# Nearest-neighbour upsampling by two: two loads instead of three, other store sizes, a first copy on one engine

## The chip, the cores and the metric

The kernel runs on one core of a Trainium2 chip. The metric is the device time of one execution in microseconds (us); for a run of several executions the median is given. Beside it there is a profile of one execution, taken by the hardware profiler, with a span of its own that is a little shorter than the measured time.

## The reference

```python
def setup_inputs():
    batch, channels, h, w = (16, 64, 64, 64)
    return {'x': np.random.randn(batch, channels, h, w).astype(np.float32), 'scale_factor': 2}

def reference(x, scale_factor):
    ...
    for i in range(new_h):
        for j in range(new_w):
            src_i = i // scale_factor
            src_j = j // scale_factor
            result[:, :, i, j] = x[:, :, src_i, src_j].copy()
    return result.astype(np.float32)
```

Each pixel of 1024 images of 64 x 64 is written four times, as a square of 2 x 2. The input has 16.78 MB, the output 67.11 MB. There is no arithmetic, only moving and repeating.

## The kernel before

**Layout.** The 65,536 input rows (64 floats, 256 bytes each) are dealt to the 128 partitions of the on-chip memory: R = 512 consecutive rows to each (L173). An input row becomes two output rows of 128 floats, 1024 bytes, so that a partition's share of the output is one contiguous piece of 512 KB in memory off the chip.

**One tile.** Everything lives in one tile `mem` (L187): the whole input `xt` at its end, 512 rows per partition, and FREE = 79 output blocks (WF = 79 x 256 elements) in front of it. Each block is one input row expanded to 256 elements. The expanded rows of a store are put either at the front of the tile (even stores) or at an address that ends where the unread input begins (odd stores, L206), over input rows that have been copied already.

**Loads.** The input comes in three transfers issued by SyncE (L195): 32 rows per partition (`HEAD`, 8 KB in a piece), 256 rows (64 KB) and 224 rows (56 KB). `begin_before_barrier` moves the first EARLY load instructions ahead of the barrier at the program's start, so that they are issued at once.

**The loop** (L204 to L216) runs over `rows`, the nine store sizes. For store n of k rows, VectorE expands the first kv rows (L213), ScalarE the rest (L214), both reading each element twice along the row and each row twice by a step of zero. SyncE issues the store (L215) once both have finished. In store 0 VectorE takes all rows but one, in the others 9/16 of them, rounded down.

**What waits for what.** All loads and stores are issued by SyncE and go through one queue, q1, in order. The copy for store n needs its input loaded, and its place free: store n-2 has used the same part of the tile, so it must have landed. An odd store's place also covers input rows, so its copy waits for earlier copies that read these. The store waits for the copies alone. While store n-1 is being written, the copy for store n can run. `close_early` arranges the wait for the last store at the end; it takes the last store's semaphore from the program and is not touched by the edit.

Of the kernel before, what the change touches and what calls it, by code (L numbers as in the profile page):

```python
# [6 lines left out]

EARLY = 3  # L10


def begin_before_barrier(nc):
# [5 lines left out]
    sp = mybir.EngineType.SP  # L19
    loads = [i for i in body.instructions if i.engine == sp][:EARLY]  # L20
    for load in loads:
# [132 lines left out]
@with_exitstack  # L154
def kernel(
    ctx: ExitStack,
    tc: tile.TileContext,
    x: bass.AP,
    scale_factor: int,
    out: bass.AP,  # L160
):
    nc = tc.nc
    nc.at_finalize(begin_before_barrier)
    nc.at_finalize(close_early)
    P = nc.NUM_PARTITIONS
    s = int(scale_factor)
    B, C, H, W = x.shape
    R = B * C * H // P
    fdt = x.dtype

    xp = x.rearrange("b c h w -> (b c h) w").rearrange("(p r) w -> p r w", p=P)  # L173
    op = out.rearrange("b c (h hd) w -> (b c h) (hd w)", hd=s).rearrange(
        "(p r) w -> p r w", p=P
    )

    rows = [54, 38, 52, 63, 52, 64, 63, 63, 63]
    GROW = s * s
    FREE = 79
    WF = FREE * GROW * W
    assert sum(rows) == R
    mem_pool = ctx.enter_context(tc.tile_pool(name="mem", bufs=1))
    mem = mem_pool.tile([P, WF + R * W], fdt, name="mem")  # L187
    xt = mem[:, WF:].rearrange("p (r w) -> p r w", r=R)

    HEAD = 32
    cuts = [0, HEAD, R // 2 + HEAD, R]
    for lo, hi in zip(cuts, cuts[1:]):
        nc.sync.dma_start(out=xt[:, lo:hi], in_=xp[:, lo:hi])  # L195

    def expanded(r0, r1):
        return (
            xt[:, r0:r1].unsqueeze(2).unsqueeze(4).to_broadcast([P, r1 - r0, s, W, s])
        )  # L200

    r0 = 0
    before = (0, 0)
    for n, k in enumerate(rows):  # L204
        size = k * GROW * W
        at = 0 if n % 2 == 0 else WF + r0 * W - size  # L206
        assert at >= before[1] or at + size <= before[0]
        before = (at, at + size)
        u = mem[:, at : at + size].rearrange(
            "p (k a w b) -> p k a w b", k=k, a=s, w=W  # L210
        )
        kv = k - 1 if n == 0 else k * 9 // 16
        nc.vector.tensor_copy(out=u[:, :kv], in_=expanded(r0, r0 + kv))  # L213
        nc.scalar.copy(out=u[:, kv:], in_=expanded(r0 + kv, r0 + k))  # L214
        nc.sync.dma_start(out=op[:, r0 : r0 + k, :], in_=u)  # L215
        r0 += k  # L216

# [34 lines left out]
```

## Time and profile before

| | |
|---|---|
| time, median of 3 runs | 197.24 us (196.97 to 197.29) |
| span of the profiled execution | 195.9 us (195.86) |
| moved by DMA | 83.89 MB, mean 428 GB/s over the span |
| load 1, 1024 KB | issued at 0.0, lands 4.8 us later |
| load 2, 8192 KB | issued at 0.43, lands 23.7 us later |
| load 3, 7168 KB | issued at 0.9, lands 40.1 us later |
| store 0, 6912 KB | issued at 38.57, lands 18.8 us later |
| VectorE (DVE) | 9 copies, 78.6 us |
| ScalarE (ACT) | 9 copies and a table load, 46.5 us |

In the profile DVE is VectorE, ACT ScalarE, POOL GpSimd and SP SyncE; SPq and DVEq are their instruction queues. A landing is the moment at which all 16 DMA engines have reported a transfer as done. A copy is named by its size, so 128x8960 is 35 rows of 256 elements on 128 partitions. The row of digits gives the busy share of each fortieth of the span in tenths, 9 for 90% or more. The chain of waits follows the execution back from its last instruction, at each step to whatever released it. DMA packets are counted in the stretch in which they begin, so that the share of a short stretch can lie above one, and that of the next one below.

### The profile page before, as it was taken

To read this page: it belongs to the slowest core of one execution; us is meant where nothing else is said; L and a number is where in the kernel's file an instruction comes from. 1 tells how busy PE (TensorE), PEld (TensorE's weight loads), DVE (VectorE), ACT (ScalarE), POOL (GpSimd) and SP (SyncE) were. 2 spreads that over 40 slices of the span, in tenths; PEclk is the share of its full clock that TensorE was granted. 3 is DMA by queue.
4 is the path that set the end of the run, shared out by engine and by line. 5 is a ranking of instruction groups with operands and counts; after the bars stand their busy time and mean duration, and the time that the engine had idled before them with its cause. 6 is when DMAs were issued, how large, how long until landed. Compare 5 with 4: busy or idle time off the path is not lost.

```text
span 195.9 us, 102 instructions
## 1 busy us (share of the span) xinstructions
DVE 78.6 (40%) x9; ACT 46.5 (24%) x10; POOL 0.2 (0%) x4
## 2 busy tenths in 40 slices
DVE  0000099990029399078008106930692079100000
ACT  2000000160027093074910006665000074000000
POOL 0000000000000000000000000000000000000000
DMA  9999989889899989899999899999999999999994
GB/s 428 428 428 428 402 375 550 386 361 542 361 435 397 540 348 522 348 422 422 448 417 500 370 500 428 428 428 428 422 422 422 435 435 514 461 435 448 435 422 211
DMA packets 1728, 83.89 MB, mean 428 GB/s; under 512 B 192, under 2 KB 192, under 8 KB 192
## 3 DMA queue, kind: packets, MB, share of 16 engines
q1 hardware_dynamic: 1728, 83.89, 99.2%
HBM read 16.78 MB, written 67.11 MB: 428 GB/s over the span
## 4 chain that ended last, share of the span: by engine, by line
DMA 60%; DVE 25%; issue 0%; SPq 0%; DVEq 0%
DMA out_dram<-mem 48%; DVE mem L213 25%; DMA mem<-in_x_dram 12%; SPq L195 0%; DVEq L213 0%; SPq L215 0%
## 5 line engine op out<-in xcount | busy, mean ns | idle before, releaser
L213 DVE COPY mem<-mem 128x8960 f32<-128x8960 f32 (+4 forms) x9 | 78.6, 8745 | 88.7 <-DMA out_dram<-mem 64.5
L214 ACT COPY mem<-mem 128x7168 f32<-128x7168 f32 (+3 forms) x9 | 45.2, 5027 | 115.6 <-DMA out_dram<-mem 74.1
L214 ACT ACT_TABLE_LOAD x1 | 1.3, 1283 | 1.7 <-PEq L233 1.7
L233 POOL MEMSET const-uint8-127<- 128x1 uint8 x1 | 0.1, 102 | 0.0
L233 POOL MEMSET const-bfloat16-1.0<- 128x1 bf16 x1 | 0.1, 101 | 0.0
L233 POOL MEMSET const-float32-0.0<- 128x1 f32 x1 | 0.1, 98 | 0.2 <-issue 0.2
L233 POOL MEMSET const-float32-1.0<- 128x1 f32 x1 | 0.1, 98 | 0.0
## 6 DMA issues: line engine op xcount, KB each, us to landing
out_dram<-mem SPq DMA_DIRECT2D x4, 8064.0 KB, 28.5
out_dram<-mem SPq DMA_DIRECT2D x2, 6656.0 KB, 22.9
mem<-in_x_dram SPq DMA_DIRECT2D x1, 7168.0 KB, 40.1
out_dram<-mem SPq DMA_DIRECT2D x1, 6912.0 KB, 18.8
out_dram<-mem SPq DMA_DIRECT2D x1, 4864.0 KB, 24.7
mem<-in_x_dram SPq DMA_DIRECT2D x1, 1024.0 KB, 4.8
mem<-in_x_dram SPq DMA_DIRECT2D x1, 23.7
out_dram<-mem SPq DMA_DIRECT2D x1, 30.0
```

Of the source, the lines that this page charges most:

```text
L213: nc.vector.tensor_copy(out=u[:, :kv], in_=expanded(r0, r0 + kv))
L214: nc.scalar.copy(out=u[:, kv:], in_=expanded(r0 + kv, r0 + k))
L233: nc = _bacc.Bacc("TRN2", target_bir_lowering=False, num_devices=1)
```

## The change

```diff
-EARLY = 3
+EARLY = 2
...
-    rows = [54, 38, 52, 63, 52, 64, 63, 63, 63]
+    rows = [60, 34, 55, 61, 55, 62, 62, 62, 61]
...
-    HEAD = 32
-    cuts = [0, HEAD, R // 2 + HEAD, R]
+    cuts = [0, R // 2, R]
     for lo, hi in zip(cuts, cuts[1:]):
         nc.sync.dma_start(out=xt[:, lo:hi], in_=xp[:, lo:hi])
...
-        kv = k - 1 if n == 0 else k * 9 // 16
+        kv = k if n == 0 else k * 7 // 16
         nc.vector.tensor_copy(out=u[:, :kv], in_=expanded(r0, r0 + kv))
-        nc.scalar.copy(out=u[:, kv:], in_=expanded(r0 + kv, r0 + k))
+        if kv < k:
+            nc.scalar.copy(out=u[:, kv:], in_=expanded(r0 + kv, r0 + k))
         nc.sync.dma_start(out=op[:, r0 : r0 + k, :], in_=u)
```

The loads become two of 256 rows per partition, 64 KB in a piece, both ahead of the barrier. The nine stores have 60, 34, 55, 61, 55, 62, 62, 62 and 61 rows. VectorE copies all 60 rows of store 0, and 14, 24, 26, 24, 27, 27, 27 and 26 rows of the others; ScalarE copies 20, 31, 35, 31, 35, 35, 35 and 35. Before, VectorE had 53, 21, 29, 35, 29, 36, 35, 35 and 35 rows, ScalarE 1, 17, 23, 28, 23, 28, 28, 28 and 28. Bytes, the order of the stores and the engine that issues them are as they were. In the changed kernel the loads stand in line 194, VectorE's copy in line 212; ScalarE's copy and the stores keep lines 214 and 215.

## The prediction

> **What bounds the kernel now.** I read the page first: its shares and slices, then the chain of waits, the copies by shape, and the transfers over short stretches.
>
> ```profile
> DVE 78.6 (40%) x9; ACT 46.5 (24%) x10; POOL 0.2 (0%) x4
> ...
> DMA  9999989889899989899999899999999999999994
> ...
> q1 hardware_dynamic: 1728, 83.89, 99.2%
> ```
>
> The compute engines work 40% and 24% of the span; the DMA engines work in all of it (99.2%), and the only low slice is the last. So the first suspicion is that the bytes set the time. The chain seems to say otherwise (25% VectorE), so I check whether a copy in it ever leaves the queue empty:
>
> ```profile
> 0.43 23.67 DMA mem<-in_x_dram
> ...
> 24.20 14.30 DVE mem L213
> ...
> 38.57 18.80 DMA out_dram<-mem
> ...
> 57.46 7.90 DVE mem L213
> ...
> 65.43 19.09 DMA out_dram<-mem
> ```
>
> Load 2 lands at 0.43 + 23.67 = 24.10. Load 1 (the issues' view: 1024 KB, 4.8 us to landing) lands at about 4.76. So 8.389 MB took 24.10 - 4.76 = 19.34 us, or 433.7 GB/s. Load 3, issued at 0.9, lands 40.1 us later, at 41.0. Store 0 was issued at 38.57 and landed at 57.37; its 7.078 MB need 16.32 us at that rate, so it moved from 41.05 on: the moment the loads ended. The VectorE link in the chain is the last condition for the issue, not for the data, which queued behind load 3. The same for store 2: issued at 65.43, 3.5 us before store 1 landed (copy 3, which waits for store 1, began at 68.97).
>
> All bytes at that rate: 83.89 MB / 433.7 GB/s = 193.43 us. Load 1 alone took 4.76 us for 1.049 MB, which need 2.42: 2.34 us are the start and the landing. 193.43 + 2.34 = 195.77 against a span of 195.86. All eleven joints between the twelve transfers thus cost about 0.1 us together, some 0.01 each. The span is start-up plus bytes. The start in short stretches (columns: stretch, length, VectorE, ScalarE, GpSimd, clock, DMA share, GB/s; a packet counts where it begins):
>
> ```profile
> 0.00:1.00 1.00, 0.00 (x0) 0.00 (x0) 0.20 (x4) 1.00 0.00 0
> 1.00:2.00 1.00, 0.00 (x0) 0.27 (x1) 0.00 (x0) 1.00 1.04 238
> ```
>
> Nothing moves in the first 1.0 us. In the next one 238 GB/s start where 433.7 would fit: (433.7 - 238) x 1 us = 0.196 MB, 0.45 us of lost flow, a ramp.
>
> **The change, part by part.** The sum is made on the span of 195.86; the median, 197.24, lies 1.38 above it, and I carry that over.
>
> *One load less.* The same 16.78 MB come in two transfers. One joint falls away: 0.01 us. The question is the ramp, since the first transfer now has rows of 64 KB instead of 8 KB, which no row shows at the start. Bounds: if the ramp belongs to the small rows, it goes, -0.45 us; if it lasts as long as each DMA engine's first row, a row of 64 KB (8.389 MB in 8 rows per engine and 19.34 us: 2.42 us each) at 238/433.7 of the rate takes 4.41 us, a loss of 2.0 instead of 0.45, +1.5 us. I take nearly the old ramp, as a thing of the first microsecond: -0.1, since in the stretch from 2 to 4 us the same small rows already flow at 528 GB/s as counted. SyncE spends 0.38 us to issue the first load and 0.43 on the others: +0.05 at most. Load 1 of the changed kernel lands at 2.34 + 19.34 = 21.7, load 2 at 41.0.
>
> *The first copy on VectorE alone, 60 rows.* It waited for loads 1 and 2 (24.10); now for load 1 only (21.7). Its duration comes from this:
>
> ```profile
> L213 DVE COPY mem<-mem 128x8960 f32<-128x8960 f32 x4 | 37.9, 9486 | 33.9 <-DMA out_dram<-mem 33.9
> ...
> L214 ACT COPY mem<-mem 128x5888 f32<-128x5888 f32 x2 | 10.2, 5098 | 24.4 <-DMA out_dram<-mem 24.4
> L213 DVE COPY mem<-mem 128x5376 f32<-128x5376 f32 x1 | 5.7, 5744 | 0.0
> L213 DVE COPY mem<-mem 128x9216 f32<-128x9216 f32 x1 | 5.0, 4961 | 11.1 <-DMA out_dram<-mem 11.1
> ```
>
> Copies of 21, 29, 35 and 53 rows fit 0.14 us + 1.043 ns an element; the one of 36 rows takes half (0.523 ns). So 60 rows (15360 elements) take 16.2 us or 8.2 us: store 0 is issued at 37.9 or 29.9, before 38.57 either way, and its data wait for load 2 until 41.0. No gain, no loss. The cover is load 2; were it gone, the copy's whole length would show.
> By the Trainium skill (VectorE: DVE Perf Modes, "What auto-detection actually checks") a one-source copy uses both ports when the outermost dimensions are even or equal; the trace agrees: only the even count, 36, is at half time. By it the copies of 60, 14, 24, 26, 24 and 26 rows run fast and VectorE's 78.6 us fall to about 46; the end stays.
>
> *ScalarE's one row goes (0.41 us), its table load moves.* The added condition leaves nine VectorE and eight ScalarE copies. The compiled order puts the wait for load 1 on the table load, so its 1.28 us come at 21.7 instead of 1.73; behind it stands only ScalarE's copy 1, which waits for VectorE's copy 0 anyway (its output covers the input rows copy 0 reads). Hidden by copy 0: 0.
>
> *New sizes and 7/16 on VectorE.* ScalarE's rows fit 0.19 us + 0.833 ns an element: 31 rows 6.8 us, 35 rows 7.7 us. VectorE's odd 27 rows take 7.35 us, so ScalarE ends most copies. Copy n+2 starts when store n lands and is covered by store n+1. The thinnest cover is store 1, now 34 rows, 4.456 MB, 10.3 us. Store 0 lands at 41.0 + 18.1 = 59.1; copy 2 ends at 59.1 + 0.1 + 6.8, store 2 is issued at 66.1, store 1 lands at 69.4: 3.3 us ahead, where 3.5 was enough before, and 2.4 (38.57 against 41.0) at store 0. Every later store has at least 8 us (copy 3: issue 77.3, store 2 lands 86.0). SyncE issues the stores in the same order, nothing is moved past another. Cost: 0.
>
> *Sum:* -0.01 - 0.1 + at most 0.05 is about -0.1: a span near 195.8 and a time of 197.1.
>
> **Rivals.**
> 1. *The ramp was the small rows'.* All of it goes: -0.46 us, 196.8. For it: the low rate is seen only in load 1, the one transfer with 8 KB rows. Against: it is also the only one that meets idle engines.
> 2. *The ramp lasts as long as the first row.* +1.5: 198.7. It decides from an excess of 0.4 us. For it: no 64 KB row ever began on idle engines here. Against: small rows reached full flow within the first few, at one time for all.
> 3. *Store 2 comes late.* Fast VectorE copies beside a ScalarE copy are not in the trace (copy 5's two parts ran at 103.63 and 92.58). Should ScalarE stand still for VectorE's 3.35 us of copy 2, it ends at 69.4 and store 2 is issued as store 1 lands. The engines then sit idle for at least the 1.0 us from issue to first packet, at most the 2.4 us proven enough: +1.4 taken, 198.5. The price starts where copy 2 exceeds about 7.7 us (0.9 us of spare cover). Against: slow VectorE copies left ScalarE alone (6.17 us beside one, 6.16 without).
> 4. *Each load pays its start again.* Then the load taken out is worth load 1's 2.34 us: 194.9. The trace speaks against it: eleven joints in 0.1 us.
> The Trainium skill (DMA: Bandwidth & Descriptors, "Anatomy of one DMA") names about 2.0 us fixed for each transfer, by which it would be about 195.2; transfers that queue behind one another do not pay it in this trace.
>
> **How the numbers follow.** Forecast 0.57, rival 1 0.19, rival 2 0.11, rival 3 0.06, rival 4 0.02, and 0.05 for a loss of unknown place. No change means within 0.2%, 0.39 us (196.85 to 197.63), about what a measurement of this kernel can tell. Forecast: same, save 0.01 on the slow side by scatter (the three runs spread over 0.32 us). Rival 1 ends on the border; I count it faster, with rival 4: 0.21. Slower: 0.11 + 0.06 + 0.05 + 0.01 = 0.23. Same: 0.56. The range: 196.5 holds rival 1 with scatter, 198.3 the smaller half of rivals 2 and 3; outside stay rival 4 and their larger half, about 0.15. The forecast's own range is 196.9 to 197.4.
>
> **What would show it.** The DMA row stays at 9 but for the ends; load 1 lands near 21.7, load 2 near 41.0; the 128x15360 copy takes 8.2 us; store 0 lands near 59.1 wherever it is issued; store 2 is issued 3 us before store 1 lands; VectorE falls to 46 us with the same span. Wrong would be: a first load landing after 22.1 (rival 2) or before 21.4 (rival 1), a ScalarE copy of 128x7936 above 7.7 us or a low DMA slice near 69 us (rival 3), or a span under 195.2.

## The result and the profile after

| | before | changed |
|---|---|---|
| time, median of 5 runs | 197.24 us (196.97 to 197.42) | 198.37 us (198.20 to 198.50) |
| span of the profiled execution | 195.86 | 196.96 |
| VectorE, ScalarE busy | 78.6, 46.5 | 46.1, 57.6 |
| first copy's input lands | 24.10 | 21.75 |
| store 0 issued, lands | 38.57, 57.37 | 29.96, 60.45 |

The ratio is 1.0057, with a 95% interval of 1.0045 to 1.0070: slower by 1.1 us, where about -0.1 was forecast and the range ended at 198.3.

The page of the changed kernel (shares, slices, queue), and the first steps of its chain of waits (start, length, what):

```profile
DVE 46.1 (23%) x9; ACT 57.6 (29%) x9; POOL 0.2 (0%) x4
...
DMA  9999999999999989889998998999999999999994
...
q1 hardware_dynamic: 1584, 83.89, 99.2%
```

```profile
0.00 21.75 DMA mem<-in_x_dram
...
21.77 8.17 DVE mem L212
...
29.96 30.49 DMA out_dram<-mem
...
60.47 6.82 ACT mem L214
...
67.31 20.05 DMA out_dram<-mem
```

By the page nothing is lost: the DMA engines are busy 99.2% of the span in both kernels, with 99.2% of a longer one here. The chain shows where the time is. Load 1 lands at 21.75 (21.7 forecast), the first copy takes 8.17 us (8.2), store 0 is issued at 29.96 (29.9). But it lands at 29.96 + 30.49 = 60.45, where the bytes give 59.1. Behind it all goes at the old rate: store 0's landing to the span's end are 136.5 us, and stores 1 to 8 have 59.24 MB, which need 136.6 at 433.7 GB/s. So the whole difference lies between load 1's landing and store 0's, in 38.7 us in which the queue was never empty.

The issue of load 2 (us from issue to landing) narrows it further:

```profile
mem<-in_x_dram SPq DMA_DIRECT2D x1, 41.9
```

Issued at 0.42, load 2 lands at 42.3 instead of 41.0 or 41.1. The load became late, not the store. The packets in stretches of 2 us around the joint of loads and stores, the kernel before first, the changed one second (stretch, length, VectorE, ScalarE, GpSimd, clock, DMA share, GB/s):

```profile
36.00:38.00 2.00, 2.00 (x1) 0.00 (x0) 0.00 (x0) 1.00 0.86 373
38.00:40.00 2.00, 2.00 (x2) 1.43 (x1) 0.00 (x0) 1.00 0.99 430
40.00:42.00 2.00, 2.00 (x1) 2.00 (x1) 0.00 (x0) 1.00 1.03 442
```

```profile
36.00:38.00 2.00, 0.00 (x0) 0.00 (x0) 0.00 (x0) 1.00 0.83 229
38.00:40.00 2.00, 0.00 (x0) 0.00 (x0) 0.00 (x0) 1.00 0.99 295
40.00:42.00 2.00, 0.00 (x0) 0.00 (x0) 0.00 (x0) 1.00 1.14 492
```

The packets that begin from 38 to 40 keep the DMA engines as busy as before (0.99), but carry 295 GB/s, not 430. The packet records behind these lines give each piece of a transfer, one partition's share of it on one DMA engine, with its start and length. Such a piece is called a row here: load 2 has 128 rows of 64 KB, eight for each engine. From 30 us on, every row of load 2 takes 2.42 or 2.43 us but the last of each engine, which takes 3.3 to 4.0. Both compute engines are idle at that time. A busy share says that packets were open, not that bytes flowed at the full rate.

### The profile page after: what moved, and what is told of

It reads as the page before. It is cut to its first block, busy times and chain, and to the rows that moved or that the text cites. A ratio compares the mean times of both kernels' runs of the same rounds, so it can differ in the third digit from the quotient of the medians.

```text
span 197.0 us, 96 instructions
## 1 busy us (share of the span) xinstructions
DVE 46.1 (23%) x9; ACT 57.6 (29%) x9; POOL 0.2 (0%) x4
## 3 DMA queue, kind: packets, MB, share of 16 engines
q1 hardware_dynamic: 1584, 83.89, 99.2%
## 4 chain that ended last, share of the span: by engine, by line
DMA 66%; ACT 15%; DVE 4%; issue 0%; ACTq 0%
DMA out_dram<-mem 55%; ACT mem L214 15%; DMA mem<-in_x_dram 11%; DVE mem L212 4%; ACTq L214 0%
## 5 line engine op out<-in xcount | busy, mean ns | idle before, releaser
L214 ACT COPY mem<-mem 128x8960 f32<-128x8960 f32 (+2 forms) x8 | 56.4, 7045 | 88.0 <-DMA out_dram<-mem 81.2
L212 DVE COPY mem<-mem 128x6912 f32<-128x6912 f32 (+4 forms) x9 | 46.1, 5135 | 117.4 <-DMA out_dram<-mem 95.6
```

## The experiments

Two things had changed at this joint: the last load's rows (64 KB instead of 56), and how long store 0 had stood in the queue when the loads ended (some 12 us instead of 2.5). Theory A blames the waiting store, theory C the loads.

To compare the runs I take one number from the chain of each: store 0's landing, less the landing that released the first copy, less the bytes between them (last load and store 0) at 433.7 GB/s. It is 57.37 - 24.10 - 33.24 = 0.03 us for the kernel before and 60.45 - 21.75 - 37.47 = 1.23 for the changed one; "the loss at the joint" below. Ratios are against the kernel before, timed on the same chip, with their 95% interval.

**1. The kernel before with a fast first copy.** Only the first copy changes, from 53 rows and 1 row to an even 54 on VectorE.

```diff
-        kv = k - 1 if n == 0 else k * 9 // 16
+        kv = k if n == 0 else k * 9 // 16
...
+        if kv < k:
```

> The kernel before, with its three loads and its sizes; only the first copy changes: all 54 rows on VectorE, an even count, so about 7.4 us instead of 14.3, and store 0 is issued near 31.6 instead of 38.57. Theory A (a store that stands in the queue well before the loads end makes the last load rows slow): load 3 lands about 1.2 us later, near 42.2, the span is near 197.1, the time near 198.4. Theory C (the loads of 64 KB rows at the end are what is slow, whenever the store is issued): load 3 lands at 41.0, span 195.9, time 197.2.

198.32 us, ratio 1.0054 (1.0039 to 1.0069). From its chain:

```profile
0.42 23.90 DMA mem<-in_x_dram
...
31.81 26.87 DMA out_dram<-mem
```

The issue of load 3 (us from issue to landing, 40.1 in the kernel before):

```profile
mem<-in_x_dram SPq DMA_DIRECT2D x1, 7168.0 KB, 41.4
```

The same loads, the same sizes, a copy that ends 7 us earlier, and load 3, issued at 0.9, lands at 42.3, where theory A had 42.2 and theory C 41.0. Store 0 lands at 58.68, not at 57.37: a loss at the joint of 1.11 us. One line of the diff accounts for nearly all of the change, and it is one that makes an engine faster.

**2. The changed kernel with a slow first copy.** The reverse.

```diff
-        kv = k if n == 0 else k * 7 // 16
+        kv = k - 1 if n == 0 else k * 7 // 16
```

> The changed kernel with its two loads and its sizes; only the first copy changes: 59 rows on VectorE, an odd count, and one row on ScalarE, so about 15.9 us instead of 8.2, and store 0 is issued near 37.7 instead of 29.96. Theory A: the last rows of load 2 take 2.4 us again, load 2 lands near 41.0, the span is near 195.8, the time near 197.1. Theory C: nothing changes, span 197.0, time 198.4.

197.69 us, ratio 1.0021 (1.0012 to 1.0030). Store 0, issued at 37.90, lands at 59.62; the loss at the joint is 0.25. This fits theory A, with a remainder: an issue 0.7 us earlier than in the kernel before still costs something. (The profiled execution, 197.46, was the fastest of the ten, so the usual loss is rather larger.)

**3. The changed kernel with three loads.** All three are issued ahead of the barrier, as in the kernel before.

```diff
-EARLY = 2
+EARLY = 3
...
-    cuts = [0, R // 2, R]
+    cuts = [0, 32, R // 2 + 32, R]
```

> The changed kernel with the three loads of before (32, 256 and 224 rows); the first copy stays fast, 8.2 us from load 2's landing at 24.1, so store 0 is issued near 32.3. Theory A: slow all the same, span near 197.0, time near 198.4. Theory C: span near 195.9, time near 197.2.

198.43 us, ratio 1.0056 (1.0039 to 1.0072), loss at the joint 1.36. Undoing the loads mends nothing; theory C falls.

**4. A small last load.** Is the last row stretched in proportion, so that a short one would cost little? Here, too, all three loads are issued ahead of the barrier.

```diff
-EARLY = 2
+EARLY = 3
...
-    cuts = [0, R // 2, R]
+    cuts = [0, R // 2, R - 8, R]
```

> The changed kernel with its second load cut into 248 rows and 8 rows (2 KB in a piece); store 0 is issued near 29.9 as before the cut. Theory A in the form that each DMA engine's last load row is stretched in proportion (3.6 us for 2.4): the last row has 2 KB now, the loss shrinks from 1.2 us to under 0.1, span near 195.9, time near 197.2. Theory A in the form of a fixed pause where loads change to stores: still 1.2 us, span 197.0, time 198.4. Theory C (a last load of 64 KB rows): no loss, as it ends in small rows, 197.2.

198.62 us, ratio 1.0062 (1.0047 to 1.0077), loss 1.65. The rows of 2 KB go at their rate, and now the row of 62 KB ahead of them takes 3.0 to 4.0 us. The loss is tied to the time just before the stores begin, not to the last piece. The form with the proportion was wrong. The loss is also 0.4 us above the changed kernel's, which no run explains.

**5 and 6. When must the store be issued?** A useless extra copy, of 25 or of 17 rows, ahead of the fast first copy moves store 0's issue, and store 1's with it, which stands behind it; loads, sizes and the other copies stay. (VectorE's copy 1 then runs ahead of copy 0 too.) The edit with 25 rows:

```diff
+        if n == 0:
+            nc.vector.tensor_copy(out=u[:, :25], in_=expanded(0, 25))
         nc.vector.tensor_copy(out=u[:, :kv], in_=expanded(r0, r0 + kv))
```

> The changed kernel with one useless extra VectorE copy of 25 rows ahead of the first copy (6.8 us; VectorE's copy 1 of 2.0 us then also runs first), so that store 0 is issued near 38.8, with fast copies as before. Theory A, by the issue time alone: the last load rows take 2.4 us again, load 2 lands near 41.0 to 41.1, span near 195.8, time near 197.2. If not the issue time but the changed sizes or the fast VectorE copy were to blame: 198.4.

> The same with 17 useless rows (4.7 us), store 0 issued near 36.7. Theory A with a loss that grows with the lead until it is full: about half of the 1.2 us, span near 196.4, time near 197.8 (0.25 us were lost with an issue at 37.9). Theory A with a threshold at the start of the last load row (about 38): the full 1.2 us, time near 198.4.

With 25 rows 197.15 us, ratio 0.9994 (0.9985 to 1.0003), the loss at the joint 0.31; with 17 rows 198.12 us, ratio 1.0042 (1.0027 to 1.0057), loss 0.86. The chain with 25 rows:

```profile
0.00 21.86 DMA mem<-in_x_dram
21.86 0.02 issue
21.88 6.82 DVE mem L213
28.70 10.01 DVE mem L214 x2
38.72 0.02 issue
38.73 20.91 DMA out_dram<-mem
```

The stretch from 38 to 40 us, to be set beside the two above:

```profile
38.00:40.00 2.00, 0.70 (x1) 1.26 (x1) 0.00 (x0) 1.00 1.23 524
```

VectorE does 6.8 us of work for nothing, store 0 goes out 8.8 us later than in the changed kernel and lands 0.8 us earlier (59.64). The packets of the stretch carry 524 GB/s at a share of 1.23, which is nearly the full rate again (524 / 1.23 = 426), where the changed kernel had 295 at 0.99. Both loads, all sizes and all fast copies of the change are still in. With run 1 this shows from both sides that the early issue is the cause; one rival, idle compute engines, is left to run 8. The 0.31 that is left is of another kind: in the packet records the last rows of load 2 take 2.43 to 2.51 us, and the rows ahead of them, begun before the store was issued, up to 2.59; why, no run shows. It need not be there in every execution: the profiled one took 197.45 us, 0.30 above the median of the ten. With 17 rows, issued at 36.78, the loss is neither full nor half; it grows over some microseconds of lead.

**7. Does the loss follow the waiting bytes?** Store 0 in two pieces, a tiny one issued early, the rest in time.

```diff
+        if n == 0:
+            nc.vector.tensor_copy(out=u[:, :2], in_=expanded(0, 2))
+            nc.sync.dma_start(out=op[:, :2, :], in_=u[:, :2])
+            nc.vector.tensor_copy(out=u[:, 2:3], in_=expanded(2, 3))
+            nc.vector.tensor_copy(out=u[:, 2:55], in_=expanded(2, 55))
+            nc.scalar.copy(out=u[:, 55:], in_=expanded(55, 60))
+            nc.sync.dma_start(out=op[:, 2:k, :], in_=u[:, 2:])
+            r0 += k
+            continue
```

> The changed kernel with store 0 in two pieces: 2 rows (2 KB in a piece, 16 KB for each DMA engine) issued near 22.3, the other 58 near 38.9. If the loss is room or transfer time taken by data of the waiting store that is read ahead: 16 KB are 0.6 us at an engine's rate, so at most half of the loss, time near 197.5 to 197.9. If the change from loads to stores costs a fixed pause wherever a store stands behind: 198.4. If a store as small as this takes no part: 197.2.

198.03 us, ratio 1.0035 (1.0022 to 1.0048). Load 2 landed at 41.75, 0.66 us late; the loss at the joint is 0.75. This lies between the two extremes, a little above the 197.5 to 197.9 of the first: a store of 1/30 of the size costs about half.

**8. Store 1 held back.** In the changed kernel store 1, too, stood in the queue when the loads ended.

```diff
+        if n == 1:
+            for _ in range(4):
+                nc.vector.tensor_copy(out=u[:, :13], in_=expanded(r0, r0 + 13))
```

> The changed kernel with store 1 held back: four useless VectorE copies of 13 rows behind copy 1 issue it near 46 instead of 34.45; store 0 stays at 29.96. If one waiting store is enough: nothing changes, span 197.0, time 198.4. If it takes both stores in the queue (the number of waiting descriptors): span near 195.8, time near 197.2.

198.40 us, ratio 1.0056 (1.0039 to 1.0073), loss 1.16, with store 1 issued at 46.6. One waiting store is enough. The run also answers the rival that was left: both compute engines were idle at the joint in the changed kernel, and one or both were busy there in the kernel before and in run 5. Here VectorE copies from 31.9 to 46.5 us, and the loss stays.

**9 and 10. One row early, four rows early**, as in 7. The number of pieces is the same in all three (8 for each engine), the bytes are not. With one row the rest is 53 rows on VectorE and 6 on ScalarE, with four 51 and 5.

> Store 0 in two pieces again: 1 row (1 KB in a piece, 8 KB for each DMA engine) issued near 22, the other 59 rows near 38.4. With 2 rows (16 KB for each engine) load 2 landed 0.66 us later than its bytes ask. If the loss follows the bytes that wait (16 KB are 0.60 us at an engine's rate): about 0.3 us, load 2 lands near 41.4. If it follows the number of waiting pieces, which is the same 8 for each engine: 0.66 us again, near 41.75.

> The same with 4 rows (4 KB in a piece, 32 KB for each engine) near 22.5 and 56 rows near 38.6. By bytes: 32 KB are 1.2 us, as much as whole stores cost; load 2 lands near 42.2, time near 198.4. By pieces: 0.66 us, near 41.75, time near 198.0.

One row: 197.51 us, ratio 1.0018 (1.0009 to 1.0027). Four rows: 198.16 us, ratio 1.0048 (1.0034 to 1.0061). The landing of load 2, by its issue in each of the two, with one row first:

```profile
mem<-in_x_dram SPq DMA_DIRECT2D x1, 41.1
```

```profile
mem<-in_x_dram SPq DMA_DIRECT2D x1, 41.8
```

It lands at 41.5, 41.75 (7) and 42.2, and the loss at the joint is 0.62, 0.75 and 1.31 for 8, 16 and 32 KB waiting at each engine; 480 KB (the whole store) cost 1.23. So the loss grows with the waiting bytes up to some 32 KB and then no further; it does not follow the number of pieces. By these landings it is not in proportion: load 2 is late by 0.53, 0.66 and 1.22 us, where the bytes alone gave 0.3, 0.6 and 1.2. But each landing is that of one execution. By the median times, each against the kernel before on the same chip, 8, 16 and 32 KB cost 0.35, 0.60 and 1.00 us and the changed kernel 1.13, which is nearer to the bytes. So the growth is shown, and the proportion stays open.

**11. Store 0 in ScalarE's queue**, not behind the loads but beside them.

```diff
-        nc.sync.dma_start(out=op[:, r0 : r0 + k, :], in_=u)
+        (nc.scalar if n == 0 else nc.sync).dma_start(out=op[:, r0 : r0 + k, :], in_=u)
```

> The changed kernel with store 0 issued by ScalarE, in a queue of its own, near 30. The DMA engines can then take it beside load 2, not behind it. If the loss comes only where a load ends with a store behind it in the same queue, it is gone or smaller, span near 195.8, time 197.2. If every change of an engine from a load's row to a store's costs, the rows that alternate cost several times over: span above 198.

205.17 us, ratio 1.0389 (1.0373 to 1.0405). Its chain and two stretches:

```profile
30.08 39.98 DMA out_dram<-mem
...
70.08 6.82 ACT mem L214
...
76.92 18.05 DMA out_dram<-mem
```

```profile
30.00:52.00 22.00, 1.99 (x2) 5.74 (x2) 0.00 (x0) 1.00 1.00 388
...
74.00:79.00 5.00, 3.63 (x1) 4.97 (x2) 0.00 (x0) 1.00 0.42 180
```

The profiled execution was the slowest of the five (206.22 us); its span, 204.9, is 9.1 us over the 195.77 of the bytes, in two parts. While the engines alternate between load and store they move 388 GB/s; over these 22 us that is 2.3 us lost against 433.7. Most of the rest is a wait. Store 0, mixed in, lands only at 70.06, and store 1, which should cover copy 2 (6.8 us), at 73.90. In the packet records all rows of store 1 but three have ended by 71.4, and the last of the three by 73.6. Store 2 is issued at 76.92, and its first rows begin at 77.8: most engines stood idle for some 6.4 us. So the second form of the expectation, a span above 198, came true, but for the smaller part by the mix itself. That the cover of copy 2 would go was not foreseen in the expectation.

**12. Store 0 later still**, 27 useless rows.

> The changed kernel with 27 useless rows (7.4 us) ahead of the first copy: store 0 is issued near 39.3, 0.5 us later than with 25. By the issue time: load 2 lands at its bytes' time, near 41.1 (0.26 us better than with 25), span near 195.8, time near 197.0, at or a little below the kernel before. If the issue is too late, the engines that end the loads first sit idle for some tenths: time near 197.4.

197.94 us, ratio 1.0036 (1.0023 to 1.0048). The chain:

```profile
0.00 22.06 DMA mem<-in_x_dram
...
39.47 20.34 DMA out_dram<-mem
```

Load 2 lands at 41.40, just the 19.34 us of its bytes behind load 1: no row is slow any more. But the engines that ended their loads first found no store yet, and store 0 lands 0.27 us behind its bytes. Load 1 came 0.3 us later than in the changed kernel, and 0.4 us more were lost after store 0 than with 25 rows (136.9 us from its landing to the span's end instead of 136.5), spread over all the stores. These two are not explained, and with them the run says less about the last tenths than was hoped. No run here is clearly faster than the kernel before; the one with 25 rows, 0.9994 (0.9985 to 1.0003), is level with it.

Put in order of store 0's issue, for a whole store 0 in the one queue: 29.96, 1.23; 31.81 (1), 1.11; 36.78, 0.86; 37.90, 0.25; 38.57 (before), 0.03; 38.73, 0.31; 39.47, 0.27 as a gap. Only at some 2.5 us ahead of the loads' end, in the kernel before and in run 5, is the time level; at 3.3 us ahead (2) it is 0.2% longer, and at 1.9 (12) 0.4%, part of which lies elsewhere. In the packet records the stores that left the last row of the loads at its rate, or nearly (before, 5, 12), were issued just after that row had begun on every engine (by 38.5 to 38.6). In run 2, where the issue at 37.90 fell on the first of these beginnings, the last rows took 2.5 to 2.9 us. Whether it is the row's beginning that counts or the lead in microseconds, no run separates.

## Why the prediction was wrong

**The bound** was read rightly: start-up plus bytes, and no compute engine in the way. The kernel stayed at the DMA engines' limit through its whole span.

**The ramp at the start** was the open question of the sum, with bounds of -0.45 and +1.5. Its size held: load 1 with rows of 64 KB landed at 21.75, 21.68 being the sum with the old ramp. The small gain of 0.1 did not show there. That the ramp is a thing of the first microsecond is not shown: in the packet records the first row of each engine took 2.7 to 3.4 us instead of 2.42, far from the 4.41 of the upper bound. Rivals 1 and 2 were both wrong.

**The first copy** was predicted to 0.03 us (8.2 us, measured 8.17), and store 0's issue to 0.06 (29.9, measured 29.96). The step that failed is the sentence behind it: store 0 "is issued at 37.9 or 29.9, before 38.57 either way, and its data wait for load 2 until 41.0. No gain, no loss." A store that waits was priced at nothing, with the load as its cover. It costs 1.2 us when it waits from 29.96 on, while the load that covers it becomes slower. Experiments 1 and 5 show it from both sides: the issue time alone adds 1.1 us to the joint of the kernel before, and takes most of the loss off the changed one's.

The trace of before could not show the price. Loads and stores meet in it once, and there the store was issued 2.5 us ahead; no row has a store that waits longer behind a load. The stores that wait behind stores (store 1, issued at 44.2 and begun at 56.4) cost nothing, and the prediction carried that over. So the step had no bounds of its own: a later issue was priced, an earlier one was not.

**The cover of store 2** held: copy 2 took 6.81 us beside a fast VectorE copy, so ScalarE was not slowed (rival 3), and the stores followed one another at the full rate. **The joints** cost nothing (rival 4): one load less gave no 2 us, and between stores the time is the bytes'.

**VectorE's even counts.** Two lines of the changed kernel, an odd count and an even one:

```profile
L212 DVE COPY mem<-mem 128x6912 f32<-128x6912 f32 x3 | 22.1, 7352 | 35.7 <-DMA out_dram<-mem 35.7
...
L212 DVE COPY mem<-mem 128x15360 f32<-128x15360 f32 x1 | 8.2, 8160 | 21.8 <-DMA mem<-in_x_dram 21.8
```

The copies of 60, 14, 24 and 26 rows took half the time an element, the three of 27 rows did not (7352 ns, 7.35 forecast); VectorE's total, 46.1 us, is the 46 forecast. This part of the prediction was right, and it is what led to the loss: the even 60 brought store 0's issue forward by 8 us.

## What to carry to other kernels

A transfer queued early is not always free: where loads hand over to stores in one queue, look at how long the first store waits behind the last load, and measure both an earlier and a later issue. An engine made faster off the critical path changes when its transfers are queued, and that can cost more than the copy ever did. A DMA share of 99% is no proof that nothing can be lost; set the bytes of a stretch against the best rate seen in the trace.

## What the runs showed of the hardware

A store waiting behind a load in the same queue slows that load's last row on every engine, from 2.42 us to 3.3 to 4.0 in the changed kernel; where the loads ended in pieces of 2 KB (4), it was the row of 62 KB ahead of them. The load lands about 1.2 us late once 32 KB or more wait at each engine, 0.66 for 16 KB and 0.53 for 8 KB in the profiled executions, and at most 0.25 us late if the store is issued some 2.5 us ahead of the loads' end. 32 KB at an engine's share of 433.7 GB/s (27.1 GB/s) are 1.2 us, which would fit an engine that reads ahead so many bytes of the store while it still writes the load, but in its profile the store of 8 KB cost more than that gives; this is argued from the sizes, and stays open. A mix costs the DMA engines too: with a store in a second queue beside a load, they moved 388 GB/s in place of 433.7.
